# A max-pool over 134 MB: one big store of the outputs, other sizes of the first and the last loads

## The chip, the cores and the metric

The kernel runs on one core of a Trainium2 chip. The metric is the device time of one execution in microseconds, lower is better; of several runs the median counts. The profile is that of one execution. Its span is the time between the first and the last thing that the profiler saw on the core.

## The reference

The input x has the shape 32 x 256 x 4096, in fp32 (134.2 MB). Every row of 4096 is cut into 256 windows of 16 values, and each output is the largest value of a window:

```python
for i in range(output_size):                       # 256
    start = int(i * length / output_size)          # length 4096
    end = int((i + 1) * length / output_size)
    result[:, :, i] = np.max(x[:, :, start:end], axis=-1)
```

There are 2,097,152 windows, 16,384 for each of the 128 partitions. The output is 8.4 MB.

## The kernel before

All windows lie one after the other in memory, so the kernel takes them in groups: in a group, partition p owns one contiguous stretch of windows, and its outputs are one contiguous stretch as well. Group A has 9,340 windows per partition, group B 7,044. A load brings the next n windows of every partition, 64 bytes a window, as one contiguous run per partition: a load of 1024 windows is 64 KB per partition, 8 MB in all.

The loads, all issued by SyncE (SP) in this order, are: one short load of 128 windows (`FIRST`, line 85), then 16 loads on line 94: eight of 1024, one of 1020, six of 1024 and at last one of 900. In the text "the last full load" is the last of 1024 windows.

The loads go into `ring`, one buffer in SBUF with room for 2 x (1024 + 152) windows: two slots of 1024 + `GAP` windows, which the loads take in turn. Within its slot, a load lies at the slot's start or is moved by `GAP` = 152 windows, and this changes every second load. The load that comes next into a slot is thus shifted by 152 windows against the one it replaces, and it needs only the 872 windows that both share to be consumed; the other 152 windows may be reduced later. Each load's reduction is split accordingly into a piece of 872 windows, which goes first, and a piece of 152 (`pooled`, line 56, on VectorE). The short first load lies at window 1024 of the ring, in the gap of the first slot.

The reductions write into `kept`, a buffer in SBUF that holds all outputs but those of the last load. The last load's outputs (900 per partition) are written into a free stretch of the ring and leave in a store of their own.

There are three stores. The outputs of group A (9,340 per partition, 37 KB runs) and those of group B without the last load (6,144, 24 KB runs) are issued by SP on line 114, after all loads; the last load's (900, 3.6 KB runs) by ScalarE's queue (ACT) on line 111. A queue takes its instructions in order. The framework orders them by the buffers they touch: a load waits until the windows that it overwrites are reduced, a reduction until its load has landed, a store until the outputs that it reads are written. `no_sync_barrier` keeps the order of the program around it and lets nothing wait.

Of the kernel before, what the change touches and what calls it, by code (L numbers as in the profile page):

```python
# [1 line left out]

# [4 lines left out]


@with_exitstack
def kernel(  # L10
    ctx: ExitStack,
    tc: tile.TileContext,
    x: bass.AP,
    output_size: bass.AP,
    out: bass.AP,
):

    nc = tc.nc
    P = nc.NUM_PARTITIONS
    fp32 = mybir.dt.float32

    B, C, L = x.shape
    O = int(output_size)  # L30
    assert L % O == 0, (L, O)
    W = L // O
    total = B * C * O // P
    assert B * C * O % P == 0

    CHUNK = 1024
    GAP = 152
    FIRST = 128
    LOADS_A, LOADS_B = 9, 6

    LESS = 4
    group_a = [FIRST] + [CHUNK] * (LOADS_A - 1) + [CHUNK - LESS]
    last = total - sum(group_a) - LOADS_B * CHUNK
    group_b = [CHUNK] * LOADS_B + [last]
    assert 0 < last and last * (W + 1) <= CHUNK * W

    pool = ctx.enter_context(tc.tile_pool(name="pool", bufs=1))
    ring = pool.tile([P, 2 * (CHUNK + GAP) * W], fp32, tag="ring", name="ring")
    kept = pool.tile([P, total - last], fp32, tag="kept", name="kept")

    xw = x.flatten_outer_dims().rearrange("r (o w) -> (r o) w", w=W)
    ow = out.flatten_outer_dims().rearrange("r o -> (r o)")

    def pooled(dst, at, n):

        nc.vector.reduce_max(  # L56
            out=dst,
            in_=ring[:, at * W : (at + n) * W].rearrange("p (n w) -> p n w", w=W),
            axis=mybir.AxisListType.X,
        )  # L60

    taken = 0

    def group(n):

        nonlocal taken
        span = slice(taken * P, (taken + n) * P)
        taken += n
        return (
            xw[span].rearrange("(p n) w -> p (n w)", p=P),  # L70
            ow[span].rearrange("(p n) -> p n", p=P),
        )

    stores = []
    n_loads = 0
    base = 0
    for g, loads in enumerate((group_a, group_b)):
        xg, og = group(sum(loads))
        a = 0
        for n in loads:  # L80
            xn = xg[:, a * W : (a + n) * W]
            dst = kept[:, base + a : base + a + n] if n != last else None
            if n == FIRST:

                nc.sync.dma_start(  # L85
                    out=ring[:, CHUNK * W : (CHUNK + n) * W], in_=xn
                )
                pooled(dst, CHUNK, n)
            else:

                low = n_loads % 2 * (CHUNK + GAP)
                moved = n_loads // 2 % 2
                at = low + moved * GAP
                nc.sync.dma_start(out=ring[:, at * W : (at + n) * W], in_=xn)
                if n != last:
                    cut = CHUNK - GAP if moved else GAP
                    parts = [(0, cut), (cut, n)]
                    for u, v in parts if moved else parts[::-1]:
                        pooled(dst[:, u:v], at + u, v - u)
                else:  # L100
                    end = (at + CHUNK) * W
                    last_kept = ring[:, end - n : end]
                    pooled(last_kept, at, n)
                n_loads += 1
            a += n
        full = a - last if g else a
        stores.append((og[:, 0:full], kept[:, base : base + full]))
        base += full
    assert taken == total

    nc.scalar.dma_start(out=og[:, full : full + last], in_=last_kept)
    tc.no_sync_barrier()
    for dst, src in stores:
        nc.sync.dma_start(out=dst, in_=src)


# [1 line left out]
_INS = ['x', 'output_size']  # L118
_OUTS = [((32, 256, 256), 'float32')]

_NUMBERS = {'output_size': 256}


# [26 lines left out]
```

## Time and profile before

| | |
|---|---|
| median of 3 runs | 334.98 us (334.89 to 335.07) |
| profiled execution, device time | 334.98 us |
| its span | 333.2 us |
| VectorE busy | 276.5 us, 83% |
| DMA, queue of SP | 2736 packets, 142.15 MB, 98.8% of 16 engines' span |
| DMA, queue of ACT | 144 packets, 0.46 MB, 0.3% |
| HBM read and written | 134.22 MB and 8.39 MB, 428 GB/s over the span |

The span is the profile's own time; the device time holds 1.8 us more around it. "Issue" is the time at which a queue hands out a DMA, "landing" the time at which its semaphore shows that all of it has arrived. The 16 DMA engines serve all queues. On the chain of work that ended last, 57.5% of the span is a wait for a load and 36.0% is reductions into kept.

### The profile page before, as it was taken

What the parts mean: (1) busy time and instruction counts of PE and PEld (TensorE: products, weight loads), DVE (VectorE), ACT (ScalarE), POOL (GpSimd) and SP (SyncE); (2) the same over time, 40 slices, a digit from 0 to 9 for tenths busy, and PEclk for the clock granted to TensorE, in tenths of its full rate; (3) what the DMA queues carried; (4) which work ended last, traced back from release to release, by engine and by line L of the source; (5) the groups of instructions that cost most, each with busy time, mean ns of one, the idle gap of its engine ahead of it and who ended that gap; (6) DMA issues with size and microseconds to landing.
All of it is one profiled execution on the core that took longest, in us unless ns stands there. A gap on an engine that the chain in (4) does not pass through costs nothing.

```text
span 333.2 us, 113 instructions
## 1 busy us (share of the span) xinstructions
DVE 276.5 (83%) x32; POOL 0.2 (0%) x4
## 2 busy tenths in 40 slices
DVE  2009979797997979799797979979797998979993
POOL 0000000000000000000000000000000000000000
DMA  9898989899898989899898989899898989899987
GB/s 378 378 504 378 504 378 504 378 409 472 378 504 378 504 378 504 378 417 464 376 502 377 504 378 496 386 425 456 378 504 378 504 378 504 378 458 443 393 386 339
DMA packets 2880, 142.61 MB, mean 428 GB/s; under 512 B 320, under 2 KB 320, under 8 KB 448
## 3 DMA queue, kind: packets, MB, share of 16 engines
q1 hardware_dynamic: 2736, 142.15, 98.8%
q10 hardware_dynamic: 144, 0.46, 0.3%
HBM read 134.22 MB, written 8.39 MB: 428 GB/s over the span
## 4 chain that ended last, share of the span: by engine, by line
DMA 57%; DVE 36%; DVEq 5%; issue 0%; SPq 0%
DMA ring<-in_x_dram 57%; DVE kept L56 36%; DVEq L145 5%; SPq L85 0%
## 5 line engine op out<-in xcount | busy, mean ns | idle before, releaser
L56 DVE TENSOR_REDUCE kept<-ring 128x152 f32<-128x2432 f32 (+3 forms) x31 | 261.4, 8473 | 51.6 <-DMA ring<-in_x_dram 51.6
L56 DVE TENSOR_REDUCE ring<-ring 128x900 f32<-128x14400 f32 x1 | 15.1, 15141 | 0.0
L131 POOL MEMSET const-bfloat16-1.0<- 128x1 bf16 x1 | 0.1, 102 | 0.0
L131 POOL MEMSET const-uint8-127<- 128x1 uint8 x1 | 0.1, 101 | 0.0
L131 POOL MEMSET const-float32-0.0<- 128x1 f32 x1 | 0.1, 99 | 0.2 <-issue 0.2
L131 POOL MEMSET const-float32-1.0<- 128x1 f32 x1 | 0.1, 98 | 0.0
## 6 DMA issues: line engine op xcount, KB each, us to landing
ring<-in_x_dram SPq DMA_DIRECT2D x1, 8160.0 KB, 24.0
ring<-in_x_dram SPq DMA_DIRECT2D x1, 7200.0 KB, 21.6
out_dram<-kept SPq DMA_DIRECT2D x1, 4670.0 KB, 32.4
out_dram<-kept SPq DMA_DIRECT2D x1, 3072.0 KB, 18.1
ring<-in_x_dram SPq DMA_DIRECT2D x1, 1024.0 KB, 4.6
out_dram<-ring ACTq DMA_DIRECT2D x1, 450.0 KB, 4.2
ring<-in_x_dram SPq DMA_DIRECT2D x14, 24.0
```

The costliest lines, as they stand in the source:

```text
L56: nc.vector.reduce_max(out=dst, in_=ring[:, at * W : (at + n) * W].rearrange("p (n w) -> p n w", w=W), axis=mybir.AxisListType.X,)
L131: nc = _bacc.Bacc("TRN2", target_bir_lowering=False, num_devices=1)
L145: with _tile.TileContext(nc) as tc:
```

## The change

It alters three things. The first load has 256 windows per partition (16 KB) instead of 128 (8 KB). All outputs but those of the last load form one group of 15,460 windows per partition, and leave in one store of 60 KB runs; the last load is a group of its own. After the first come 14 loads of 1024, then one of 868 (`NEXT`, 54 KB per partition) and one of 924 (58 KB); the load of 868 is reduced in one piece.

```diff
-    FIRST = 128
-    LOADS_A, LOADS_B = 9, 6
+    FIRST = 256
+    FULL = 14
 
-    LESS = 4
-    group_a = [FIRST] + [CHUNK] * (LOADS_A - 1) + [CHUNK - LESS]
-    last = total - sum(group_a) - LOADS_B * CHUNK
-    group_b = [CHUNK] * LOADS_B + [last]
-    assert 0 < last and last * (W + 1) <= CHUNK * W
+    NEXT = 868
+    group_a = [FIRST] + [CHUNK] * FULL + [NEXT]
+    last = total - sum(group_a)
+    assert 0 < last <= CHUNK and last <= GAP * W
...
-    for g, loads in enumerate((group_a, group_b)):
+    for g, loads in enumerate((group_a, [last])):
         xg, og = group(sum(loads))
         a = 0
         for n in loads:
             xn = xg[:, a * W : (a + n) * W]
-            dst = kept[:, base + a : base + a + n] if n != last else None
-            if n == FIRST:
+            dst = kept[:, a : a + n] if g == 0 else None
+            if g == 0 and a == 0:
...
                 nc.sync.dma_start(out=ring[:, at * W : (at + n) * W], in_=xn)
-                if n != last:
+                if n == CHUNK:
                     cut = CHUNK - GAP if moved else GAP
                     parts = [(0, cut), (cut, n)]
                     for u, v in parts if moved else parts[::-1]:
                         pooled(dst[:, u:v], at + u, v - u)
+                elif g == 0:
+                    pooled(dst, at, n)
                 else:
-                    end = (at + CHUNK) * W
-                    last_kept = ring[:, end - n : end]
+
+                    free = low if moved else at + CHUNK
+                    last_kept = ring[:, free * W : free * W + n]
                     pooled(last_kept, at, n)
                 n_loads += 1
             a += n
-        full = a - last if g else a
-        stores.append((og[:, 0:full], kept[:, base : base + full]))
-        base += full
+        if g == 0:
+            first_og = og
     assert taken == total
 
-    nc.scalar.dma_start(out=og[:, full : full + last], in_=last_kept)
+    nc.scalar.dma_start(out=og, in_=last_kept)
     tc.no_sync_barrier()
-    for dst, src in stores:
-        nc.sync.dma_start(out=dst, in_=src)
+    nc.sync.dma_start(out=first_og, in_=kept)
```

More of the change, by code (lines that the diff above doesn't have):

```diff
@@ L72, in group @@
         )
-    stores = []
     n_loads = 0
-    base = 0
-    for g, loads in enumerate((group_a, group_b)):
+    for g, loads in enumerate((group_a, [last])):
         xg, og = group(sum(loads))
```

## The prediction

> **What bounds the kernel now.** I read the page first: its engine rows, its DMA row and its queue table, for what is busy nearly all the time.
>
> ```profile
> span 333.2 us, 113 instructions
> ...
> DVE 276.5 (83%) x32; POOL 0.2 (0%) x4
> ...
> DMA  9898989899898989899898989899898989899987
> ...
> q1 hardware_dynamic: 2736, 142.15, 98.8%
> q10 hardware_dynamic: 144, 0.46, 0.3%
> ```
>
> The two queues together keep all 16 DMA engines at work for 99.1% of the span, 330.2 of 333.2 us. What is left, 3.0 us, can be placed with the trace's packet records: the first packet starts at 1.74 us and the last ends at 331.83, 1.4 us before the end. From the fourth transfer on, an engine goes from one transfer to the next within 3 ns. So a transfer made earlier or later gains nothing in itself. The time changes only if bytes or their pace change, if an engine runs out of packets, or if the two ends move.
>
> The end needs the timeline, read with the list of DMA issues (size, then us from issue to landing).
>
> ```profile
> 276.41 17.28 DVE L56 TENSOR_REDUCE kept<-ring 128x872 f32<-128x13952 f32 x2 [2.07 <-DMA ring<-in_x_dram]
> 291.50 21.91 SPq L114 DMA_DIRECT2D out_dram<-kept  x2
> 295.75 17.28 DVE L56 TENSOR_REDUCE kept<-ring 128x872 f32<-128x13952 f32 x2 [2.07 <-DMA ring<-in_x_dram]
> 312.95 15.14 DVE L56 TENSOR_REDUCE ring<-ring 128x900 f32<-128x14400 f32 x1
> 328.12 0.37 ACTq L111 DMA_DIRECT2D out_dram<-ring  x1
> ```
>
> ```profile
> ring<-in_x_dram SPq DMA_DIRECT2D x1, 7200.0 KB, 21.6
> out_dram<-kept SPq DMA_DIRECT2D x1, 4670.0 KB, 32.4
> out_dram<-kept SPq DMA_DIRECT2D x1, 3072.0 KB, 18.1
> ring<-in_x_dram SPq DMA_DIRECT2D x1, 1024.0 KB, 4.6
> out_dram<-ring ACTq DMA_DIRECT2D x1, 450.0 KB, 4.2
> ```
>
> The reader is to see three things. The 4670 KB store is issued at 291.50, 21 us before the last load has landed, so it lies ready behind that load. The 3072 KB store follows at 313.1 and also finds a full queue. The last reduction (to 328.09) runs beside these stores; its own small store, issued at 328.12, lands at 332.3 and only then lets the kernel end. By the packet records the small store's first packet starts at 330.36, exactly as an engine finishes the stores: it waited for the queue, not for VectorE.
>
> The prices of VectorE come from the groups with shapes kept apart (busy us, mean ns).
>
> ```profile
> L56 DVE TENSOR_REDUCE kept<-ring 128x872 f32<-128x13952 f32 x14 | 205.6, 14686 | 44.3 <-DMA ring<-in_x_dram 44.3
> L56 DVE TENSOR_REDUCE kept<-ring 128x152 f32<-128x2432 f32 x15 | 40.1, 2676 | 0.0
> L56 DVE TENSOR_REDUCE ring<-ring 128x900 f32<-128x14400 f32 x1 | 15.1, 15141 | 0.0
> L56 DVE TENSOR_REDUCE kept<-ring 128x868 f32<-128x13888 f32 x1 | 14.6, 14620 | 2.0 <-DMA ring<-in_x_dram 2.0
> L56 DVE TENSOR_REDUCE kept<-ring 128x128 f32<-128x2048 f32 x1 | 2.3, 2286 | 5.4 <-DMA ring<-in_x_dram 5.4
> ```
>
> From 872 and 152 windows: (14686 - 2676) / 720 = 16.7 ns per window. For the loads: starts of the big reductions at 24.75 and 295.75 lie 14,332 windows apart, 18.91 ns each, so a load of 1024 takes 19.36 us (8.39 MB, 433 GB/s), one of 868 16.41, one of 924 17.47, and 128 windows 2.42. VectorE is faster than the loads and waits about 2.1 us for each.
>
> **What the Trainium skill says.** "DMA: Bandwidth & Descriptors", Specifications, puts the fabric ceiling at 435 GB/s and the first byte of a DMA from SP or ACT at about 0.6 us. The trace agrees with both: 433 GB/s, and the first issue ends at 1.11 us with its first packet at 1.74, 0.63 later. The same page, Issuing engines are not separate DMA queues, is borne out by the small store that waits behind SP's. "VectorE: DVE Perf Modes", The perf-mode tier table, gives the reduction only the 1x mode; 16.7 ns for 16 elements at 0.96 GHz is that. No mode helps.
>
> **The change part by part.**
>
> First load, 256 windows for 128. It lands at 5.40 + 2.42 = 7.8, its reduction takes 2.29 + 128 x 16.7 ns = 4.4 and ends at 12.2. As 256 exceeds GAP, it reaches into the second slot, and SP's third load now waits for that reduction, with SP's later loads behind it. But the second load's data run until 24.3 + 2.4 = 26.7: the wait has 14 us of cover. Cost nothing; all later loads land 2.42 later. The load of 1020 becomes 1024: another 0.08 later. Both are taken back by the shorter load 868. Bytes are the same.
>
> The last load is issued when the 872-window reduction of the last full load is done. That load lands at 276.41 + 2.50 = 278.91, its reduction ends at 293.60, and SP issues the last load at 293.61. Ahead of it in the queue lies the load of 868, which lands at 278.91 + 16.41 = 295.32. The lead is 1.7 us, where before it was 4.6 (291.1 against 295.75). A landing shows about 0.45 us after the slowest engine's last packet, and the engines are up to 0.5 us apart (packet records of the load before it: 294.79 to 295.29), so they run dry between 294.34 and 294.83. The new load's packets come, by the first load's price (0.73 to 1.74), 1.01 us after its issue: 294.62. This is just in time. Some engines are idle for up to 0.28 us, and one that stood empty starts slower: the kernel's first packets took 0.73 us, the next ones 0.31, so 0.42 more. The slowest engine, which sets the end, resumes as if at 294.62 + 0.42 = 295.04, 0.2 us late. Below, the cost is nothing (an early issue wins nothing in a full queue); above, it is the small store's 328.12 to 330.36, 2.24 us from issue to packet, most of which was queue. That bound gives 293.61 + 2.24 + 0.42 - 294.83 = 1.44. I take 0.2.
>
> The reduction of 868 must wait for the 152-window piece before it: 293.60 + 2.68 = 296.28, then 14.62 to 310.90. The big store waits on SP for this; nothing but the end is behind it there. It is issued at 310.92, its packets come at 311.93 by the same price. Before it, the engines finish the last load at 312.0 to 312.4, plus the 0.2: covered by some 0.2 to 0.5 us. If only the store took 2.24 us, it would cost 313.16 - 312.4 = 0.8 for the slowest engine; if the load did too, the load would end later and cover it. I take nothing.
>
> The stores themselves: two of 37,360 and 24,576 byte runs take 8 x (1.383 + 0.914) = 18.38 us per engine (packet records). One of 61,840 byte runs at the loads' pace (65,536 bytes in 2.418 us) takes 8 x 2.282 = 18.25. Gain 0.13; between 0 and 0.2, since the pace per byte differs by only 0.6% between 24 and 64 KB.
>
> The last reduction, 924 for 900: 15.14 + 24 x 16.7 ns = 15.54. It starts when the load lands, 312.8 + 0.2 = 313.0, and ends at 328.5. Its store is issued 0.4 us later than before, but the engines have the big store until 330.4 to 330.8, so even 2.24 us from the issue hide. The small store grows from 1.14 to 1.17 us: 0.03. If its 4.2 us to landing were all its own, 328.6 + 4.2 = 332.8 against 332.3, 0.5 later; the packet that starts as the queue ends speaks against it.
>
> Sum: +0.2 - 0.13 + 0.03 = +0.1. The profiled execution took 334.98 us with a span of 333.2, 1.78 around it, and equals the median of the three runs. Forecast: 335.1.
>
> **The rivals.** Forecast: the engines stay full, the order of equal bytes changes, 334.6 to 335.6. A difference of 0.2% (0.67 us) is about what a measurement of this kernel can tell from no change.
>
> Slower, a late last load: the wait on VectorE leaves a 1.7 us lead, and the queue runs dry at 294.8. It decides from an issue-to-packet time above 1.6 us (1.6 + 0.42 - 1.22 = 0.8, less 0.1). At 2.24 the sum is 1.44 - 0.1 = 1.3, 336.3. For it: no load of before had so short a lead, and the only warm issue seen took up to 2.24. Against: the first load's 1.01. The store on SP running dry alone, 335.7, lies at its edge.
>
> Faster, longer runs: stores of 60 KB runs would have to save over 0.67 of 18.4 us, 4%, to show; 334.2. The packet paces leave 0.2. Hardly.
>
> The tail on VectorE: the small store's latency sets the end, 335.4; same side as the forecast.
>
> It doesn't do what it says: if the big store also waited for the last reduction it would start at 328.5, 16 us late, 351. The last reduction writes into the ring, not into kept, so SP has no cause to wait for it.
>
> **How the numbers follow.** Forecast and VectorE tail 0.67 (0.57 and 0.10); late load or store 0.26; waiting for the last reduction 0.01; faster 0.06. The range reaches from 334.6 to the late load's 336.3. Faster 0.06, same 0.67, slower 0.27.
>
> **What would show it.** Right: DMA engines busy about 330 us, SP's store issued near 310.9 and landing near 331.2, the last load landing near 313.0, the small store's issue near 328.5 and its landing near 332.4. Wrong: a last load that lands over 0.7 us later than 312.8, a store whose packets start later than the load's last ones end, or a small store that lands well after the big one with the engines idle between them.

## The result: 0.5% slower, and the profile after

The changed kernel takes 336.74 us (median of 6 runs, 336.31 to 337.73) against 335.02 for the kernel before on the same chip (6 runs, 334.89 to 335.38): a ratio of 1.0052, with a 95% interval of 1.0037 to 1.0067. That is 1.7 us. The forecast was 335.1 and its range went to 336.3, so the forecast was wrong; what happened is the slower rival, the late last load.

The page of the changed kernel, in the same rows as for the kernel before:

```profile
span 334.8 us, 113 instructions
...
DVE 276.4 (83%) x31; POOL 0.2 (0%) x4
...
DMA  9898989898999989898989899998989899989996
...
q1 hardware_dynamic: 2592, 142.13, 98.5%
q10 hardware_dynamic: 144, 0.47, 0.4%
```

The same bytes need nearly the same busy time: 98.9% of 334.8 us is 331.1 us of 16 engines, 330.2 before. The engines now have 0.9 us more of busy time and 0.7 us more of idle time, and the span is 1.6 us longer. The profiled execution took 336.61 us, 1.63 more than that of before.

The end, from the timeline (start us, us, engine, line, what; idle before it in brackets):

```profile
278.99 31.80 DVE L55 TENSOR_REDUCE kept<-ring 128x872 f32<-128x13952 f32 x3 [2.08 <-DMA ring<-in_x_dram]
293.70 0.33 SPq L91 DMA_DIRECT2D ring<-in_x_dram  x1
310.82 0.35 SPq L112 DMA_DIRECT2D out_dram<-kept  x1
314.35 15.55 DVE L55 TENSOR_REDUCE ring<-ring 128x924 f32<-128x14784 f32 x1 [3.56 <-DMA ring<-in_x_dram]
329.94 0.37 ACTq L110 DMA_DIRECT2D out_dram<-ring  x1
```

and the DMA issues (KB, us from issue to landing):

```profile
out_dram<-kept SPq DMA_DIRECT2D x1, 7730.0 KB, 21.7
ring<-in_x_dram SPq DMA_DIRECT2D x1, 7392.0 KB, 20.6
ring<-in_x_dram SPq DMA_DIRECT2D x1, 2048.0 KB, 7.3
out_dram<-ring ACTq DMA_DIRECT2D x1, 462.0 KB, 4.0
```

The row at 314.35 holds the result. The last load is issued at 293.70 (forecast 293.61), the big store at 310.82 (310.92), both as worked out. But the last load lands at 314.3 and not at 313.0: VectorE, which before went from the last full load's pieces straight into the last reduction, waits 3.56 us for it. What comes after is 1.3 to 1.5 us later than forecast.

The packet records (start and length of each packet) say what the engines did there. Each row below is one engine: two packets of 55,552 bytes of the load of 868 windows, then the first four of 59,136 bytes of the last load, whose usual length is 2.18 us. Four of the 16 rows:

```
start of the row, then lengths in us (gap = idle before the packet)
290.21: 2.05 2.06 (gap 0.96) 3.33 2.19 2.18 2.19
290.43: 2.05 2.06 (gap 0.13) 3.05 2.19 2.18 2.19
290.50: 2.05 2.06 (gap 0.06) 3.22 2.18 2.18 2.18
290.69: 2.05 2.06            3.48 2.18 2.18 2.18
```

The records do not name the engine. A packet that follows a gap was put to the engine that had become free last before it, so which engine had which gap is not shown. The mean does not hang on this: over all engines the idle time is 0.26 us, and the first packet takes 2.93 us instead of 2.18. Nor does the last row, where the packets follow each other within 0.01 us: this engine had no idle time and yet the longest first packet.

The slowest engine ends the last load at 313.91 (312.40 before: +1.51), the big store at 332.14 (18.23 us later; 18.31 before for two stores: -0.08), the small store at 333.52 (1.38 us later; 1.12 before: +0.26). The sum is +1.69.

### The profile page after: what moved, and what is told of

It is laid out like the page before. It is cut to its first block, busy times and chain, and to the rows that moved or that the text cites. A ratio compares the mean times of both kernels' runs of the same rounds, so it can differ in the third digit from the quotient of the medians.

```text
span 334.8 us, 113 instructions
## 1 busy us (share of the span) xinstructions
DVE 276.4 (83%) x31; POOL 0.2 (0%) x4
## 4 chain that ended last, share of the span: by engine, by line
DMA 61%; DVE 37%; issue 0%; DVEq 0%
DMA ring<-in_x_dram 61%; DVE kept L55 32%; DVE ring L55 5%; DVEq L55 0%
## 5 line engine op out<-in xcount | busy, mean ns | idle before, releaser
L55 DVE TENSOR_REDUCE kept<-ring 128x872 f32<-128x13952 f32 (+3 forms) x30 | 260.8, 8736 | 49.9 <-DMA ring<-in_x_dram 49.9
L55 DVE TENSOR_REDUCE ring<-ring 128x924 f32<-128x14784 f32 x1 | 15.6, 15552 | 3.6 <-DMA ring<-in_x_dram 3.6
```

What stands on the lines that cost most here:

```text
L55: nc.vector.reduce_max(out=dst, in_=ring[:, at * W : (at + n) * W].rearrange("p (n w) -> p n w", w=W), axis=mybir.AxisListType.X,)
```

## The experiments

Three theories were put against each other. Theory 1: the last load is issued too late, with 1.7 us of data ahead of it, and the engines start it from an empty queue. Theory 2: the one store that must wait for all reductions costs the time. Theory 3: the last load is slow by where it lies, a group of its own. The base in every comparison is the kernel before, 335.02 us (335.00 in the last pair).

**Two stores again (two_stores).** The changed kernel, but the first part of the outputs can leave early:

```diff
-    nc.sync.dma_start(out=first_og, in_=kept)
+    half = FIRST + 9 * CHUNK
+    nc.sync.dma_start(out=first_og[:, 0:half], in_=kept[:, 0:half])
+    nc.sync.dma_start(out=first_og[:, half:], in_=kept[:, half:])
```

> The changed kernel with its big store cut in two: 9,472 windows per partition (37 KB runs), whose outputs are ready long before, and the other 5,988 (24 KB runs). The first is issued right behind the last load, near 294.0 us, so it lies in the queue; the sizes of the loads stay. Theory 1, the last load is issued too late and the engines run dry ahead of it: the loss stays, 336.5 to 336.9, the last load lands near 314.2 again. Theory 2, the one store that waits for all reductions costs the time: it goes back to 335.0 to 335.3. Theory 3, the last load is slow by where its data lie (a group of its own): as theory 1.

338.30 us, ratio 1.0101 (1.0086 to 1.0117): slower than the change itself. Theory 2 falls; theories 1 and 3 stand, and something is added that none of them named. The timeline shows where:

```profile
293.77 0.33 SPq L91 DMA_DIRECT2D ring<-in_x_dram  x1
294.15 0.42 SPq L113 DMA_DIRECT2D out_dram<-kept  x1
310.89 0.34 SPq L114 DMA_DIRECT2D out_dram<-kept  x1
316.18 15.55 DVE L55 TENSOR_REDUCE ring<-ring 128x924 f32<-128x14784 f32 x1 [5.32 <-DMA ring<-in_x_dram]
```

The last load lands at 316.2, 1.8 us later still. By the packet records not only its first packet is long (2.96) but its eighth and last as well, 2.9 to 4.0 us on every engine, where the changed kernel has 2.2 on 13 of 16. The store is queued behind it from 294.6 on. More of this below.

**One store with the old sizes of the loads (old_sizes).**

```diff
-    FIRST = 256
-    FULL = 14
-    NEXT = 868
-    group_a = [FIRST] + [CHUNK] * FULL + [NEXT]
+    FIRST = 128
+    FULL = 15
+    group_a = [FIRST] + [CHUNK] * FULL
```

> The changed kernel's one store with the load sizes of before: 128, then 15 of 1024 (each reduced in two pieces), then 896 as a group of its own. The last load has its old lead of 4.6 us, the store is issued only when the last full load is reduced, near 313.1, after the last load's data have come. Theory 1: the last load lands at 312.8 as before; the store finds an empty queue, its packets start at 314.1 against 312.0 to 312.4, so 1.7 to 2.1 us of idle engines and perhaps 0.5 for a start: 336.7 to 337.6, with the loss all after the last load. Theory 2: the same time, so this run alone doesn't tell these apart, but it gives the price of a late store. Theory 3: the last load lands late, at 314 or so.

336.61 us, 1.0044 (1.0031 to 1.0057). Its timeline:

```profile
295.71 17.28 DVE L54 TENSOR_REDUCE kept<-ring 128x872 f32<-128x13952 f32 x2 [2.07 <-DMA ring<-in_x_dram]
312.90 15.08 DVE L54 TENSOR_REDUCE ring<-ring 128x896 f32<-128x14336 f32 x1
313.01 0.35 SPq L111 DMA_DIRECT2D out_dram<-kept  x1
```

The last load is in time (VectorE doesn't wait before 312.90), and the store, issued at 313.01, finds idle engines: 2.05 us of gap in the mean. Its packets have nearly their usual length, 2.32 us for the first against 2.29, so the 0.5 us for a start that I expected isn't there. So one store with the old sizes costs as much as the change does, at another place: the sizes do take this gap away, and bring the other.

**The last load in two halves (split_last).** All of the change stays, addresses and the one store too, but the first half of the last load needs only part of the reduction:

```diff
-                nc.sync.dma_start(out=ring[:, at * W : (at + n) * W], in_=xn)
+                mid = last // 2
+                for u, v in [(0, mid), (mid, n)] if g else [(0, n)]:
+                    nc.sync.dma_start(
+                        out=ring[:, (at + u) * W : (at + v) * W],
+                        in_=xn[:, u * W : v * W],
+                    )
...
+                    if n_loads == FULL - 1:
+                        mid = GAP + last // 2
+                        parts = [(0, GAP), (mid, n), (GAP, mid)]
```

> The changed kernel with its last load issued as two halves of 462 windows, and the 872-window piece of the last full load reduced as 462 and 410: the first half needs only the 462 and is issued near 286.9, the second near 293.8 with 8.7 us of data ahead of it. Group, addresses and the one store stay; one more DMA and one more reduction (0.1 us each). Theory 1: the queue never runs dry, the last load lands near 313.0, the store's packets come near 312.0, just in time; 335.0 to 335.4. Theory 2: stays at 336.5 or more, with the gap ahead of the store. Theory 3: stays at 336.5 or more, with the last load's packets slow.

335.23 us, 1.0006 (0.9998 to 1.0014): as the kernel before. Timeline:

```profile
278.92 31.86 DVE L55 TENSOR_REDUCE kept<-ring 128x462 f32<-128x7392 f32 x4 [2.06 <-DMA ring<-in_x_dram]
286.80 7.22 SPq L93 DMA_DIRECT2D ring<-in_x_dram  x2
310.81 0.35 SPq L120 DMA_DIRECT2D out_dram<-kept  x1
312.93 15.55 DVE L55 TENSOR_REDUCE ring<-ring 128x924 f32<-128x14784 f32 x1 [2.14 <-DMA ring<-in_x_dram]
```

The first half goes out at 286.80. VectorE's wait falls from 3.56 to 2.14 us, the last reduction starts at 312.93. The store, issued at the same 310.81, comes just in time: a gap of 0.01 us in the mean. Theories 2 and 3 fall: same store, same group, no loss. What differs is the early issue, and that the load comes in two halves with packets of half the size; the next runs change the time of an issue and no packet.

**The price of a late load by itself (mid_76, mid_swap, mid_16, mid_late).** The kernel before, with nothing changed at its ends; only the reduction of the sixth full load is reordered (in two of the runs with a short reduction added), so that the load that takes its place is issued later. In mid_swap the 152-window piece goes first, in mid_76 half of it; mid_16 and mid_late put a spare reduction of 16 or 80 windows ahead of it, whose result is overwritten later. mid_16 and mid_76:

```diff
+                    if n_loads == 5:
+                        parts = parts[::-1]
+                        pooled(kept[:, 12000 : 12000 + 16], at, 16)
```

```diff
+                    if n_loads == 5:
+                        parts = [(76, cut), (cut, n), (0, 76)]
```

> The kernel before, with one load in the middle of the run made late: the sixth of the 1024-window loads is reduced with its 152-window piece first, after a spare reduction of 16 windows into a place of kept that is written again later; so the load that replaces it is issued 2.68 + 0.41 us later, with a lead of 1.6 us instead of 4.65. Theory 1: a lead that short costs the same anywhere: engines idle for up to 0.4 us, then a slow restart; that load and all after it come 1.0 to 1.5 us later, 336.0 to 336.5. Theories 2 and 3: nothing at the end or in the layout is changed, so at most the 0.0 to 0.4 us of idle engines: 335.0 to 335.4.

> The kernel before, with one load in the middle late by one reduction of 76 windows (the sixth full load is reduced as 76, 872, 76): lead 3.2 us instead of 4.65. Its packets are known to the engines some 1.8 us before the slowest engine is done. Theory A, an engine fetches ahead only while it still works on the packet before, so the price is a hidden start of about 0.75 us that comes out when the lead is too short: nothing lost here, 335.0 to 335.2. Theory B, an engine must know its next packet a whole packet (2.4 us) ahead: part of the start comes out already, 335.3 to 335.8.

> The same with the 152-window piece first: lead 1.97 us. The new packets are known 0.5 us before the slowest engine is done, about when the fastest is done. Theory A: half of the start is hidden, no engine or hardly one idle, 335.4 to 336.2. Theory B: the whole start comes out, as with the lead of 1.6: 336.2 to 336.7. A theory in which only idle time counts: 335.0 to 335.1.

> The same with a spare reduction of 80 windows as well: lead 0.5 us. All engines are empty when the packets come, for 0.5 to 1.0 us. Theories A and B: the start of 0.75 us whole, and the idle time on top: 336.9 to 337.7, 1.0 us over the lead of 1.6 at most. If the start were paid only by engines that were caught at work, less than with the lead of 1.6 plus 1.0.

The lead is read from the timeline, from the issue of the load to the landing of the one ahead of it (start of the next reduction of 872 windows). In the kernel before it is 140.94 - 136.28 = 4.66 us, in mid_late 140.85 - 140.20 = 0.65 us:

```profile
136.28 19.70 SPq L94 DMA_DIRECT2D ring<-in_x_dram  x2
140.94 17.28 DVE L56 TENSOR_REDUCE kept<-ring 128x872 f32<-128x13952 f32 x2 [2.10 <-DMA ring<-in_x_dram]
160.41 14.69 DVE L56 TENSOR_REDUCE kept<-ring 128x872 f32<-128x13952 f32 x1 [2.19 <-DMA ring<-in_x_dram]
```

```profile
140.20 15.69 SPq L94 DMA_DIRECT2D ring<-in_x_dram  x2
140.85 17.28 DVE L56 TENSOR_REDUCE kept<-ring 128x872 f32<-128x13952 f32 x2 [0.67 <-DMA ring<-in_x_dram]
162.21 14.69 DVE L56 TENSOR_REDUCE kept<-ring 128x872 f32<-128x13952 f32 x1 [4.08 <-DMA ring<-in_x_dram]
```

The late load lands at 162.2; in the kernel before it lands at 160.4. All five, with the packets of the late load from the packet records (usual length 2.42 us). "Late" is how much later than in the kernel before the slowest engine ends that load, and the last load:

| kernel | lead, us | idle engines, mean us | its first packet, mean us | late after it, us | late after the last load, us | time, us | ratio to before |
|---|---|---|---|---|---|---|---|
| before | 4.66 | 0.00 | 2.42 | | | 335.02 | |
| mid_76 | 3.33 | 0.00 | 2.50 | 0.65 | 0.57 | 335.61 | 1.0016 (1.0009 to 1.0023) |
| mid_swap | 2.03 | 0.00 | 2.78 | 0.43 | 0.92 | 335.93 | 1.0027 (1.0016 to 1.0037) |
| mid_16 | 1.73 | 0.10 | 3.02 | 0.64 | 1.12 | 336.68 | 1.0047 (1.0035 to 1.0059) |
| mid_late | 0.65 | 1.12 | 3.07 | 1.79 | 2.29 | 337.26 | 1.0068 (1.0055 to 1.0081) |

The start of a load has a price of its own, up to some 0.65 us in the mean, that is hidden as long as the queue is well ahead and comes out little by little as the lead shrinks. In mid_swap no engine is idle and the load is still late. The time holds more than this price: in mid_swap, mid_16 and mid_late some 0.5 us of the loss arises at the end of the run, where the last load hands over to the stores (see "What stays open"). The profiled execution of mid_16 took 336.06 us, the fastest of its five, so its packets explain some 1.1 us of its loss and not the median's 1.7. That this median equals the loss of the changed kernel is therefore in part chance.

Neither of the two forms of theory 1 hits every dose: mid_76 is in B's range and above A's, mid_swap in A's and below B's, and mid_16 lies 0.2 us above its range; mid_late is in its range. In mid_76 only 4 of 16 engines have a long first packet (2.5 to 3.0), but an engine that lost 0.5 us keeps it to the end of the run: its engines end the last load between 312.05 and 312.97, those of the kernel before between 312.00 and 312.40. The slowest one sets the time.

**Two halves and two stores (split_two).** split_last with the stores of two_stores.

> The last load in two halves, the first early, and the big store in two, of 9,472 and 5,988 windows, the first queued right behind the last load. With the late load these two stores were 1.6 us slower than the one. If that came from the store's packets lying behind a load that starts slowly, it is gone: 335.0 to 335.3, as the kernel before, which has the same order. If two stores with these addresses are slower in themselves: 336.5 or more.

335.10 us, 1.0002 (0.9994 to 1.0011). The extra loss of two_stores is gone once the load ahead of the stores is in time. The stores' addresses and their number cost nothing.

**Other sizes of the last two loads (next_932, next_804).** One number is changed, `NEXT = 932` or `NEXT = 804` instead of 868.

> The changed kernel with 932 windows in the load before the last and 860 in the last. The last load's lead grows from 1.7 to 2.9 us; the one-piece reduction of 932 takes 1.07 us longer, so the big store is issued at 311.9 and its packets come from 312.9 on, when the last load's data have all come (by 312.9 at the latest). If a late load costs its start and a late store only the idle time (theory 1, with the doses of the runs in the middle): the load loses 0.3 to 0.6, the store 0.2 to 0.6 us, 335.6 to 336.2, less than the 336.74 of 868 windows. If a late store costs as much as a late load: 336.7 or more.

> The other way: 804 windows in the load before the last and 988 in the last. The lead of the last load falls to 0.5 us, as in the run in the middle with that lead; the store is issued 1.07 us earlier and lies in the queue. Theory 1: the idle time of 1.1 us a mean engine is added to the start, and the last reduction ends 1.1 us later for its size, beside the store: 337.5 to 338.2. Theory 2, the late store is what costs: its issue is earlier, so less than 336.74.

932 windows: 336.35 us, 1.0049 (1.0036 to 1.0061), a little above my range and not clear of the 336.74 of 868. The lead of 2.9 us brings the first packets down (2.25 us in the mean, 2.03 usual), but the store was issued at 312.56, not at 311.9; half of this is that the load of 932 landed only 0.34 us after VectorE was free. The engines idle 1.1 us ahead of the store. 804 windows: 338.97 us, 1.0118 (1.0102 to 1.0133), 0.8 above my range, with the store issued earlier than in any other run with one store:

```profile
293.68 0.33 SPq L91 DMA_DIRECT2D ring<-in_x_dram  x1
309.73 0.35 SPq L112 DMA_DIRECT2D out_dram<-kept  x1
316.75 16.62 DVE L55 TENSOR_REDUCE ring<-ring 128x988 f32<-128x15808 f32 x1 [7.04 <-DMA ring<-in_x_dram]
333.39 0.37 ACTq L110 DMA_DIRECT2D out_dram<-ring  x1
```

The engines idle 1.53 us in the mean ahead of the last load, and its last packet, with the store queued behind it, takes 2.9 to 3.7 us (2.33 usual) as in two_stores. The longer last reduction adds to it: the small store is issued only at 333.39, and the engines idle 0.94 us in the mean ahead of it. With one big store and one last load, no size tried here gives both transfers their lead: what NEXT gives to the load it takes from the store.

## Why the prediction was wrong, point by point

- **What bounds the kernel: right.** The engines are full to the ends. Every loss found here came from idle engines or long packets.
- **First load and the new wait on it: right, to 0.3 us.** It landed at 8.07 (7.8) and its reduction took 4.42; the wait had its cover.
- **The issue times: right.** 293.70 and 310.82, within 0.1 us; 1.7 us of lead for the last load.
- **The last load's start: the step that failed.** It was taken at 0.2 us with an upper bound of 1.44; the last load ended 1.1 us late in the mean over the engines and 1.5 on the slowest, nearly all of it in its first packets and the gap ahead of them. Three things in it were wrong. The 0.42 us for a start came from the kernel's first packets of 8 KB; the first packet of the last load lost 0.75, and the 16 KB first load of this kernel 0.65 (1.26 against 0.61). I let only engines pay that had run empty; all 16 paid here (2.67 us at the least), and in mid_swap all 16 with no idle engine at all. And 1.01 us from issue to packet is that of the first engine (0.96 here); in mid_late the 16 engines start 0.96 to 1.88 us after the issue.
- **The bound of 2.24 us, and with it the rival's 336.3: a right sign from a wrong term.** The rival "a late last load" came true, but the packets came after 1.0 us, as the forecast had it. The loss lay in how slowly they then ran.
- **The big store's wait: right, but for a reason not given.** Cover was there, with the engines gapless between load and store, since the load was late. In split_last, with the load in time, it is just in time as worked out. Issued 2.1 us later, in old_sizes, it leaves a gap of 2.05 us.
- **The stores' own time: right.** -0.08 us against -0.13.
- **The small store: 0.03 forecast, 0.26 measured.** Its first packets take 0.39 us in the mean instead of 0.14. It was issued 1.0 us before the first engine was done with the big store, and not 2.2 as before; in split_last it was 1.6 us ahead and took 0.42, in old_sizes over 4 us ahead and took the usual 0.14. The lead alone does not decide, though: at 1.7 us (split_two) and 1.6 us (mid_76) the first packet also has its usual length. The packets ahead of it last 0.9 us in these two and 2.3 us in the changed kernel and in split_last; whether this makes the difference was not tested.

**What stays open.** In two_stores and next_804 the last packet of the late load is about 1 us too long; both have a store in the queue behind it. A timely load with a store behind it loses 0.1 us there (the kernel before) or nothing (split_two). Three of the runs with a late load in the middle (mid_swap, mid_16, mid_late) lose some 0.5 us at this handover too, though their last load is in time; mid_76 does not. In the changed kernel 3 of 16 engines show it (2.5 to 2.8 us), and they are among the last to finish. That the handover to a store is dear after a load that started late is seen in five runs; why, none of them tells. Nor was a lead tried against loads of other packet sizes, so whether it counts in microseconds or in packets is not shown.

## What to carry to other kernels

Where transfers fill the time, don't ask whether an engine becomes idle, but how far ahead of the queue's end the next transfer is issued: here 4.7 us of lead cost nothing, 3.3 us cost 0.6 and 1.7 us cost 1.7, a part of it at a later handover. A wait that is moved under such a lead is not hidden just because the work behind it is; split the first transfer behind the wait so that a part of it can go early. And sum up per engine, not in the mean: the slowest of 16 sets the end, and keeps its delay.

## What the runs showed of the hardware

- The first packet of a load that starts from an empty or nearly empty queue takes longer than the ones after it, in the mean by 0.75 us in the changed kernel (59 KB packets), by 0.60 in mid_16 and 0.65 in mid_late (64 KB). At the start of the program (the 16 longest packets of the first load) it is 0.65 us for 16 KB in the changed kernel, 0.48 to 0.58 in the five others with that load, and 0.43 us for 8 KB in the kernel before, 0.30 to 0.34 in five others. Not every engine pays: the one that started last in mid_late, 1.88 us after the issue, took its usual 2.42 us. A store's first packet after a gap of 2.05 us takes only 0.03 us longer (old_sizes). The Trainium skill's 0.6 us to the first byte ("DMA: Bandwidth & Descriptors", Specifications) agrees with the first engine (0.96 us after the issue begins, 0.63 after it ends).
- ACT's small store was not mixed in between the packets of SP's store: issued at 328.01 in old_sizes, its first packet starts at 332.21, as the first engine is done with all of SP's store, though the packets ahead of it are only 2.3 us long.
